# A transformer trunk kernel: narrow and small loads moved to ScalarE's queue, forget logits moved into the gate projection, more warm-up products

## Chip, cores and metric

The kernel runs on one core of a Trainium2 chip. The metric is the device time of one execution in microseconds (us), from its start to its end on that core; the number compared is the median of several runs.

## What is computed

Two layers work on 256 tokens of 2048 channels in float32. The first is attention with a forget gate, the second a causal convolution of 31 taps with layer norm; both have a SiLU gate and a residual. The change touches only the start of the first layer and when the second layer's small parameters are loaded.

```python
proj = h @ w_in                      # h: normed x, w_in: [2048, 4 * 2048 + 16]
q, k, v, gate, f_logit = split(proj) # four blocks of 2048 columns, and 16 forget columns, one a head
log_f = log_sigmoid(f_logit + b_f)
c = cumsum(log_f, axis=1)            # running sum over the tokens
s = q @ k.T * scale + c[:, None] - c[None, :]     # per head, causal
o = softmax(s) @ v
h = h + (o * silu(gate)) @ w_out
```

## The kernel before

Products are made with weights as the stationary operand, 128 x 128, and activations of 256 tokens as the moving one. To keep float32 accuracy each weight tile and each activation tile is split into an upper part (`hi`, ScalarE, L93) and a remainder (`lo`, VectorE or GpSimd, L94), and three products are added: hi*ah, hi*al, lo*ah (L161 with the channels of the result on the partition, L188 to L190 with tokens on it).

Weights come as tiles of 1 MB, 128 partitions x 2048 numbers in runs of 2 KB (`weight_tile`, L105), through SP's queue, into three buffers in turn. A tile's transfer is issued when the `lo` split of the tile that held its buffer is done. Four tiles make a projection of 512 columns, that is four heads. For the first four heads the projections come in the order K, Q, gate, V; below their tiles are called k0 to k3, q0 to q3, g0 to g3 and v0 to v3. A projection has 16 k-tiles, four in a weight tile; a k-tile of K, Q or gate is 12 products.

TensorE runs in the order of the program. Other work is put between the projections' products by an agenda: `at(n, f)` calls `f` n k-tiles later ("step"). In a stretch at the start ScalarE, VectorE and SP are in program order too; outside it these engines are ordered by a planner when the program is built.

At the start `warm_up(n)` puts n float32 products of a matrix of ones on TensorE while x and the first weights are under way. K follows, piece by piece, with the transposes of x between. Then, still in the part that is written out by hand, SP issues q0, the 16 forget columns (`fst`, 2048 rows of 64 bytes), the forget bias (`bf`), four parameter vectors (`prm`), and q1. ScalarE splits q0, sums squares of x, splits q1, and sums squares again; from these come the rows' scales `r0` and, by `row_scales` at step 8 of Q, the tile `rb`.

`load_par` transposes `prm` on TensorE (used by the second layer only). `forget_logits` splits `fst` into `fw`, makes 32 products with it (L396, L397) and scales and biases the result (`zt`). Three steps later `forget_gates` transposes `zt` (`pz`, L409) and computes log-sigmoid on GpSimd in a chain of some 25 small operations, two of them powers (L426, L428), which ends in four copies to `lfn` (L442). `forget_sums` makes the running sums on TensorE (`pc`, L450), split into `chi` and `cc`; GpSimd makes of them `la` and `rbh` (L479 to L482), which the scores of the first head (L485) need right after V.

```python
at(8, load_par)                       # step 8 of Q
at(8, lambda: row_scales(r0, ...))    # step 8 of Q
at(10, forget_logits)                 # step 10 of Q; forget_gates three steps later
...
sil = gate_group(hg)                  # the gate projection
at(4, forget_sums)                    # step 4 of V
```

Of the kernel before, what the change touches and what calls it, by code (L numbers as in the profile page):

```python
# [27 lines left out]
def tile_hybrid_trunk(  # L28
# [28 lines left out]
    # pools that live for a part of the kernel only  # L57
# [21 lines left out]
    # residual stream with the channel on the partition: hT[:, channel tile, token]  # L79
# [16 lines left out]
    def weight_tile(wv, c0, width, g, pieces=1, pool=None):  # L96
        """DMA of kg k-tiles of a column block, [128, kg * width] = 1 MB."""
# [12 lines left out]
    def split_tile(raw, width, lo_engs, hi=None, lo=None):  # L110
        """Exact halves of a weight tile, a piece for each engine in lo_engs."""
# [27 lines left out]
    # work that is interleaved with the projections: (step, function), a step being 12 products of 256 rows  # L139
# [12 lines left out]
    def products_t(ps, kt, hv, lv, ah, al, nts, by_pass=False):  # L152
        """Adds the products of k-tile kt to the given n-tiles of (x @ w)^T."""
# [15 lines left out]
    def proj_t(wv, c0, width, ah, al, lo_engs, pieces=1, banks_apart=False, ahead=False, made=()):  # L169
        """Banks of (x @ w)^T: two n-tiles of [128, 256 tokens] a bank."""  # L170
        ps = banks_t(width)
        tail = []
        for kt, hv, lv in stream(wv, c0, width, lo_engs, pieces, ahead, made):
            if banks_apart and kt >= KT - 2048 // width:
                # the banks end one after the other
                products_t(ps, kt, hv, lv, ah, al, range(2))
                tail.append((kt, hv, lv))
            else:
                products_t(ps, kt, hv, lv, ah, al, range(width // P))
# [4 lines left out]
    def products_n(ps, kt, hv, lv, ah, al, m, first, last):  # L184
        """Adds the products of k-tile kt to the rows of token block m of x @ w."""
# [9 lines left out]
    def rsqrt_mean(ssum, name, eps):  # L195
        """(ssum / D + eps) ** -0.5 for [P, 2]."""
# [9 lines left out]
    # ================= layer 0: forgetting attention =================  # L206
# [14 lines left out]
    def split_act(kt, layer, hi_t, lo_t, src):  # L221
        """Exact halves of channel tile kt times its norm gain."""
# [17 lines left out]
    with tc.manual_schedule(engines={mybir.EngineType.Activation, mybir.EngineType.DVE, mybir.EngineType.SP}):  # L240
# [30 lines left out]
        warm_up(6)  # L271
# [5 lines left out]
        warm_up(2)  # L277
# [30 lines left out]
        # gate weights of the forget logits and their bias  # L308
        fst = ph.tile([P, S], F32, tag="la", name="fst").rearrange("p (k h) -> p k h", h=H)
        nc.sync.dma_start(fst, w_fin[:, :, 4 * D : 4 * D + H])  # L310
        bf = const.tile([P, 1], F32, name="bf")
        nc.gpsimd.memset(bf, 0.0)
        nc.sync.dma_start(bf[0:H], fox_b_f[0].rearrange("(h o) -> h o", o=1))  # L313

        # the rest of the per-channel parameters, channel on the partition
        nc.sync.dma_start(prm[32:80], conv_b_in[0].rearrange("(k p) -> k p", p=P))
        nc.sync.dma_start(prm[80:96], conv_dw_b[0].rearrange("(k p) -> k p", p=P))
        nc.sync.dma_start(prm[96:112], conv_ln_g[0].rearrange("(k p) -> k p", p=P))
        nc.sync.dma_start(prm[112:128], conv_ln_b[0].rearrange("(k p) -> k p", p=P))
# [16 lines left out]
        square_sums(1)  # L336
        ss0 = sm.tile([P, 2], F32, tag="ss", name="ss0")
# [3 lines left out]
    # causal mask for the two diagonal blocks, in the sign of the negated scores  # L341
# [12 lines left out]
    # tri[t, tok block, u] = 1 where token (block * 128 + t) <= u  # L354
# [20 lines left out]
    at(8, load_par)  # L375
# [14 lines left out]
    def forget_logits():  # L390
        fw = hip.tile([P, 2048], F32R, tag="hi", name="fw")[:, 0 : 2 * KT * H].rearrange("p (k c) -> p k c", k=KT)
        split(fw[:, :, 0:H], fw[:, :, H : 2 * H], fst, nc.vector)
        # both halves of the weights in one product: rows h and H + h add up to head h
# [11 lines left out]
    def forget_gates(zt):  # L405
        """log(sigmoid(forget gate)) for [128 tokens, token block, head]."""
# [7 lines left out]
        # log sigmoid(z) = min(z, 0) - log1p(e), e = exp(-|z|), log1p(e) = 2 artanh(e / (2 + e))  # L414
# [23 lines left out]
        # each head in every quarter of the columns  # L438
# [7 lines left out]
    def forget_sums():  # L446
        """Running sums over the tokens, one product with a triangle of ones, split into exact halves."""
# [3 lines left out]
        # the upper half in quarters 0 and 2 of the partitions, the lower one in 1 and 3  # L451
# [7 lines left out]
    # head selectors: sel[p, h] = 1 where p % 32 == h  # L459
# [5 lines left out]
    def attend(hd, qT, kT, vN, sil, t0, t1, t2):  # L465
        """One head: scores and their softmax, its transpose, and the weighted values."""
# [471 lines left out]
```

## Time and profile before

| what | value |
|---|---|
| median of 3 runs | 928.78 us (928.64, 928.78, 932.81) |
| span of the profiled execution | 931.1 us |
| TensorE matmul busy in it | 889.7 us, 96% |
| VectorE busy | 634.3 us, 68% |
| ScalarE busy | 413.5 us, 44% |
| GpSimd busy | 373.9 us, 40% |

The profiled execution has no time of its own beside its span; it lies between the runs' lowest and highest, 2.3 us over their median. Busy shares are means over the whole span, and the change acts in the first 118 us, where transfers, splits and products take turns in setting the pace. Times in the rows are counted from the span's start.

### The profile page before, as it was taken

The numbers are of one execution on the slowest core, as the hardware profiler recorded it, in microseconds if no ns is written. First come the engines' busy times: TensorE is split into PE (matmuls) and PEld (weight loads), VectorE is DVE, ScalarE is ACT, GpSimd is POOL, SyncE is SP. The second block draws the span as 40 slices with busy tenths as digits, with TensorE's granted clock in tenths as the row PEclk, the third lists the DMA queues.
The fourth block names the chain that finished last, engine by engine and source line by source line (L and its number), as shares of the span: only waits on it lengthen the run. The fifth ranks groups of instructions, "written<-read, shape, count | busy, mean of one in ns | idle before, by whom it ended". The sixth has DMA issues, their size and how long they took to land.

```text
span 931.1 us, 15879 instructions
## 1 busy us (share of the span) xinstructions
PE 889.7 (96%) x6642; PEld 856.5 (92%) x6642; DVE 634.3 (68%) x1026; ACT 413.5 (44%) x535; POOL 373.9 (40%) x240
## 2 busy tenths in 40 slices
PE   8899999999999999999999999999889999588996
PEld 8899899989999999989999999999789999477886
DVE  5464564445544554456556889999999999898551
ACT  4453564346434553454445434432434443366531
POOL 3129252103410241022000487888599688622110
PEclk9999999999999999999999999999899999799999
DMA  9999965689798656654456554565355465325532
GB/s 212 169 181 177 244 180 158 182 171 182 145 179 191 177 146 179 186 207 141 150 173 179 190 182 157 164 223 165 107 181 182 136 209 172 119 89 186 178 134 91
DMA packets 101564, 157.71 MB, mean 169 GB/s; under 512 B 4740, under 2 KB 42740, under 8 KB 101364
## 3 DMA queue, kind: packets, MB, share of 16 engines
q1 hardware_dynamic: 101156, 155.63, 62.0%
q8 instruction: 52, 0.85, 0.4%
q10 hardware_dynamic: 336, 1.07, 0.3%
q14 instruction: 20, 0.16, 0.1%
HBM read 154.59 MB, written 2.10 MB: 168 GB/s over the span
## 4 chain that ended last, share of the span: by engine, by line
PE 62%; DVE 29%; issue 2%; DMA 2%; SPq 2%; POOL 1%; ACT 1%; POOLq 0%; DVEq 0%; ACTq 0%
PE pt L161 42%; DVE acc L697 19%; DVE upad L687 4%; PE pv L188 3%; PE pv L190 3%; PE pv L189 3%; PE po L189 2%; PE po L190 2%; PE po L188 2%; DMA raw<-in_fox_w_in_dram 1%; SPq L313 1%; DMA xn<-in_x_dram 1%; PE sc L485 1%; DVE t L780 1%; PE ptr L514 1%
## 5 line engine op out<-in xcount | busy, mean ns | idle before, releaser
L161 PE MATMUL pt<-ah,lo 128*128 128x256 f32 x1472 | 421.2, 286 | 10.4 <-POOL lo L94 9.9
L161 PE MATMUL pt<-ah,hi 128*128 128x256 f32 x1472 | 423.7, 288 | 3.8 <-ACT hi L93 3.8
L161 PE MATMUL pt<-al,hi 128*128 128x256 f32 x1472 | 420.4, 286 | 0.0
L93 ACT ACTIVATE hi<-raw 128x2048 fp32r<-128x2048 f32 (+2 forms) x188 | 271.0, 1464 | 294.2 <-PE pt L161 164.1
L94 DVE TENSOR_TENSOR lo<-raw,hi 128x2048 fp32r<-128x2048 f32 (+1 forms) x136 | 216.3, 1613 | 199.9 <-ACT hi L93 199.9
L161 PEld LDWEIGHTS pt<-ah,lo 128*128 128x128 f32 x1472 | 286.0, 194 | 11.6 <-POOL lo L94 10.7
L161 PEld LDWEIGHTS pt<-ah,hi 128*128 128x128 f32 x1472 | 286.3, 195 | 4.3 <-ACT hi L93 4.2
L161 PEld LDWEIGHTS pt<-al,hi 128*128 128x128 f32 x1472 | 286.4, 195 | 0.0
L94 POOL TENSOR_TENSOR lo<-raw,hi 128x2048 fp32r<-128x2048 f32 (+1 forms) x52 | 223.5, 4318 | 72.8 <-ACT hi L93 72.2
L697 DVE SCALAR_TENSOR_TENSOR acc<-upad,dwT,acc 128x256 f32<-128x256 f32 x480 | 195.7, 477 | 1.4
L161 PE MATMUL pt<-yh,hi 128*128 128x256 f32 x256 | 73.3, 286 | 0.0
L161 PE MATMUL pt<-yl,hi 128*128 128x256 f32 x256 | 72.5, 283 | 0.6 <-POOL yl L94 0.6
L161 PE MATMUL pt<-yh,lo 128*128 128x256 f32 x256 | 72.5, 283 | 0.0
L479 POOL CAST la<-ones 64x256 fp32r<-64x256 f32 x16 | 6.3, 393 | 142.8 <-PE sc L488 138.5
L188 PE MATMUL pv<-hi,ah 128*128 128x512 f32 x128 | 50.1, 391 | 0.0
L161 PEld LDWEIGHTS pt<-yl,hi 128*128 128x128 f32 x256 | 49.1, 192 | 0.8 <-POOL yl L94 0.8
L189 PE MATMUL pv<-hi,al 128*128 128x512 f32 x128 | 49.8, 389 | 0.0
L190 PE MATMUL pv<-lo,ah 128*128 128x512 f32 x128 | 49.8, 389 | 0.0
L161 PEld LDWEIGHTS pt<-yh,hi 128*128 128x128 f32 x256 | 49.1, 192 | 0.0
L161 PEld LDWEIGHTS pt<-yh,lo 128*128 128x128 f32 x256 | 49.1, 192 | 0.0
L687 DVE SCALAR_TENSOR_TENSOR upad<-ea,par,sig 128x256 f32<-128x256 f32 x16 | 39.4, 2497 | 0.4 <-ACT sig L686 0.3
L94 POOL TENSOR_TENSOR yl<-y,yh 128x256 fp32r<-128x256 f32 x15 | 19.8, 1322 | 42.1 <-ACT yh L93 42.1
(240 smaller groups left out, 1030.0 us busy)
## 6 DMA issues: line engine op xcount, KB each, us to landing
raw<-in_fox_w_in_dram SPq DMA_DIRECT2D x60, 1024.0 KB, 6.3
raw<-in_conv_w_in_dram SPq DMA_DIRECT2D x48, 1024.0 KB, 5.2
raw<-in_fox_w_out_dram SPq DMA_DIRECT2D x16, 1024.0 KB, 5.1
raw<-in_conv_w_out_dram SPq DMA_DIRECT2D x16, 1024.0 KB, 5.1
rawk<-in_fox_w_in_dram SPq DMA_DIRECT2D x4, 512.0 KB, 12.2
xn<-in_x_dram SPq DMA_DIRECT2D x3, 512.0 KB, 11.7
rawk<-in_fox_w_in_dram SPq DMA_DIRECT2D x4, 256.0 KB, 7.5
raw<-in_fox_w_in_dram SPq DMA_DIRECT2D x2, 512.0 KB, 15.2
```

Of the source, the lines that this page charges most:

```text
L93: nc.scalar.activation(dst_hi, src, AF.Copy)
L94: lo_eng.tensor_tensor(dst_lo, src, dst_hi.bitcast(F32), op=ALU.subtract)
L161: nc.tensor.matmul(ps[nt // 2][:, (nt % 2) * S : (nt % 2 + 1) * S], w[:, nt * P : (nt + 1) * P], a(kt), start=(kt == 0 and i == 0 and nt % ...
L188: nc.tensor.matmul(ps, ah(kt)[:, ms], hv, start=first, stop=False)
L189: nc.tensor.matmul(ps, al(kt)[:, ms], hv, start=False, stop=False)
L190: nc.tensor.matmul(ps, ah(kt)[:, ms], lv, start=False, stop=last)
L313: nc.sync.dma_start(bf[0:H], fox_b_f[0].rearrange("(h o) -> h o", o=1))
L485: nc.tensor.matmul(sc[:, 0:S], qT[q][:, j, :], kT[k][:, j, :], start=(i == 0), stop=False)
L514: nc.tensor.transpose(out=pt[:, dst * P : (dst + 1) * P], in_=p[:, srcs * P : (srcs + 1) * P], identity=ident)
L687: nc.vector.scalar_tensor_tensor(u[:, TAPS - 1 :], a, bT[:, ct : ct + 1], sig, op0=ALU.add, op1=ALU.mult)
L697: nc.vector.scalar_tensor_tensor(acc, src, w, negs if t == 0 else acc, op0=ALU.mult, op1=ALU.add)
L780: nc.vector.tensor_tensor(t, dall[:, cs, :], rlb.broadcast_to([P, 2, S]), op=ALU.mult)
```

## The change

- `warm_up(6)` becomes `warm_up(8)`, and `warm_up(2)` becomes `warm_up(5)`.
- The loads of `bf`, of the four parts of `prm` and of `fst` leave SP's queue, where they stood between q0 and q1. ScalarE issues them now, after the second pair of its sums of squares, with `fst` last.
- `forget_logits` is moved from step 10 of Q to step 4 of the gate projection; `forget_gates` stays three steps behind it. `load_par` is moved from step 8 of Q to step 14 of the gate projection. `forget_sums` is moved from step 4 of V to step 6.
- Comments are removed; lines that hold only that are left out below.

```diff
-        warm_up(6)
+        warm_up(8)
...
-        warm_up(2)
+        warm_up(5)
...
         q_raw = [weight_tile(w_fin, 0, 512, 0)]
         fst = ph.tile([P, S], F32, tag="la", name="fst").rearrange("p (k h) -> p k h", h=H)
-        nc.sync.dma_start(fst, w_fin[:, :, 4 * D : 4 * D + H])
         bf = const.tile([P, 1], F32, name="bf")
         nc.gpsimd.memset(bf, 0.0)
-        nc.sync.dma_start(bf[0:H], fox_b_f[0].rearrange("(h o) -> h o", o=1))
-        nc.sync.dma_start(prm[32:80], conv_b_in[0].rearrange("(k p) -> k p", p=P))
-        nc.sync.dma_start(prm[80:96], conv_dw_b[0].rearrange("(k p) -> k p", p=P))
-        nc.sync.dma_start(prm[96:112], conv_ln_g[0].rearrange("(k p) -> k p", p=P))
-        nc.sync.dma_start(prm[112:128], conv_ln_b[0].rearrange("(k p) -> k p", p=P))
         q_raw.append(weight_tile(w_fin, 0, 512, 1))
...
         square_sums(1)
+        nc.scalar.dma_start(bf[0:H], fox_b_f[0].rearrange("(h o) -> h o", o=1))
+        nc.scalar.dma_start(prm[32:80], conv_b_in[0].rearrange("(k p) -> k p", p=P))
+        nc.scalar.dma_start(prm[80:96], conv_dw_b[0].rearrange("(k p) -> k p", p=P))
+        nc.scalar.dma_start(prm[96:112], conv_ln_g[0].rearrange("(k p) -> k p", p=P))
+        nc.scalar.dma_start(prm[112:128], conv_ln_b[0].rearrange("(k p) -> k p", p=P))
+        nc.scalar.dma_start(fst, w_fin[:, :, 4 * D : 4 * D + H])
...
-    at(8, load_par)
...
-            at(10, forget_logits)
...
         qk_evict(qT, ps, -float(P) ** -0.5)
+        if hg == 0:
+            at(4, forget_logits)
+            at(14, load_par)
         sil = gate_group(hg)
         if hg == 0:
-            at(4, forget_sums)
+            at(6, forget_sums)
```

## Rows read from the trace of the kernel before

**Rows 1.** The page: each engine's busy time, share of the span and instructions.
```profile
PE 889.7 (96%) x6642; PEld 856.5 (92%) x6642; DVE 634.3 (68%) x1026; ACT 413.5 (44%) x535; POOL 373.9 (40%) x240
```

**Rows 2.** Busy time by stretch: PE, PEld, DVE, ACT, POOL, granted clock, DMA share, GB/s.
```profile
36.00:39.00 3.00, 2.46 (x18) 2.05 (x17) 2.04 (x4) 2.70 (x5) 0.00 (x0) 1.00 0.17 26
...
56.00:94.70 38.70, 38.70 (x325) 38.34 (x324) 18.84 (x23) 14.65 (x16) 27.49 (x39) 1.00 1.02 179
94.70:117.40 22.70, 22.70 (x103) 18.78 (x102) 13.95 (x10) 11.98 (x10) 4.32 (x5) 1.00 0.99 254
117.40:931.00 813.60, 779.45 (x5879) 752.19 (x5877) 572.92 (x938) 358.40 (x456) 328.94 (x170) 0.98 0.58 165
```

**Rows 3.** SP's queue in order of time: start, us, queue, line, operation, tile.
```profile
21.53 1.30 SPq L310 DMA_DIRECT2D fst<-in_fox_w_in_dram  x1
22.88 13.20 SPq L313 DMA_DIRECT2D bf<-in_fox_b_f_dram  x1
...
38.05 1.81 SPq L105 DMA_DIRECT2D raw<-in_fox_w_in_dram  x3
```

**Rows 4.** ScalarE in order of time: splits of q0, q1, g0, g1; one sum of squares.
```profile
36.30 2.19 ACT L93 ACTIVATE hi<-raw 128x512 fp32r<-128x512 f32 x4 [3.32 <-DMA raw<-in_fox_w_in_dram]
...
46.31 2.19 ACT L93 ACTIVATE hi<-raw 128x512 fp32r<-128x512 f32 x4 [5.74 <-DMA raw<-in_fox_w_in_dram]
48.41 1.04 ACT L326 ACTIVATE junk<-xn 128x1024 f32<-128x1024 f32 x1
...
63.70 1.92 ACT L93 ACTIVATE hi<-raw 128x2048 fp32r<-128x2048 f32 x1 [1.29 <-DMA raw<-in_fox_w_in_dram]
69.82 1.91 ACT L93 ACTIVATE hi<-raw 128x2048 fp32r<-128x2048 f32 x1 [4.20 <-DMA raw<-in_fox_w_in_dram]
```

**Rows 5.** TensorE in order of time, between q0's last product and q1's first.
```profile
43.21 0.28 PE L161 MATMUL pt<-ah,lo 128*128 128x256 f32 x1
46.99 0.39 PE L161 MATMUL pt<-ah,hi 128*128 128x256 f32 x1 [3.50 <-ACT hi L93]
```

**Rows 6.** Busy time in a stretch of q1, columns as in rows 2.
```profile
47.70:51.20 3.50, 3.48 (x17) 3.48 (x18) 2.10 (x5) 2.88 (x6) 0.14 (x1) 0.52 1.04 180
```

**Rows 7.** TensorE's groups in 1:8 and in 8.4:13.6: busy us, mean ns, idle before.
```profile
L269 PE MATMUL warm<-ones 128*128 128x128 f32 x16 | 4.0, 431 | 1.1 <-POOL ones L73 1.1
...
L161 PE MATMUL pt<-ah,hik 128*128 128x256 f32 x8 | 2.3, 433 | 0.0
```

**Rows 8.** The chain of work in 40:72: start, us, what.
```profile
55.38 0.21 DVE dg_l L236
...
56.12 2.88 PE pt L161 x24
...
62.63 4.31 PE pt L161 x36
66.95 0.24 PE pz L409 x2
```

**Rows 9.** VectorE in order of time: remainder of g0.
```profile
65.65 2.29 DVE L94 TENSOR_TENSOR lo<-raw,hi 128x2048 fp32r<-128x2048 f32 x1 [0.97 <-ACT hi L93]
```

**Rows 10.** GpSimd in order of time: forget gates, and the first head's operands.
```profile
69.43 5.46 POOL L426 TENSOR_TENSOR fg<-fg 128x32 f32<-128x32 f32 x1
...
89.19 0.66 POOL L442 COPY lfn<-fg 128x32 f32<-128x32 f32 x4
...
113.74 0.41 POOL L482 CAST rbh<-ones 64x256 fp32r<-64x256 f32 x1
```

**Rows 11.** The chain of work in 0:160, V's start to the first scores.
```profile
94.74 0.23 PE pv L188
...
100.21 0.86 PE pc L450 x4
...
117.44 0.35 PE sc L485 x3
```

**Rows 12.** DMA issues in 0:100: times, KB, median us from issue to landing.
```profile
fst<-in_fox_w_in_dram SPq DMA_DIRECT2D x1, 128.0 KB, 15.6
```

## Prediction

> **What bounds the kernel now.** I read the page's busy times first, then busy time by stretch, then SP's, ScalarE's, TensorE's and GpSimd's instructions in order of time, and the chain of work. TensorE is busy for 96% of the span [rows 1]. After the first V projection it is busy for 779 of 814 us [rows 2], and nothing there is changed; all that work hangs on its predecessors and on no fixed time. So the change is worth what it does to the start of the first scores, 117.44 us [rows 11].
>
> Up to there two paces compete. One is TensorE: 24 products take 2.88 us [rows 8], so 0.12 us each, 1.44 us a k-tile, 5.76 us a weight tile. The other is the transfers. The splits of q1 and g1 both start as their data lands, 46.31 and 69.82 [rows 4]: four tiles in 23.5 us, 5.88 us a tile. The DMA engines show a share of 1.02 from 56 to 94.7 us at 179 GB/s [rows 2]. The paces are within 2%, so a lead of TensorE over its data isn't kept for long: what counts is whether the transfers start sooner.
>
> They do stop once. SP issues fst, and its next issue, bf, takes 13.20 us [rows 3]; four small loads follow, and q1 is issued at 38.05, after the split of q0 has begun at 36.30 [rows 4]. In 36 to 39 us the DMA engines' share is 0.17 [rows 2]. TensorE then idles 3.50 us before q1 [rows 5], and in the 3.5 us from 47.70 the granted clock is 0.52, the lower of its two levels, with 17 products where the full clock would make 29 [rows 6].
>
> **The small loads leave SP's queue.** q1 is then issued as soon as its buffer is free, before q0 has landed. q0 itself doesn't land sooner: fst stood behind it in the same queue. So q1's data comes one tile after q0's, 36.30 + 5.88 = 42.2, which is 4.1 earlier. The transfer of fst is still to be made, somewhere behind q1. It landed at 21.53 + 15.6 = 37.1 [rows 3, 12], 0.8 after q0; as some of it lay beside q0, I take 1.0 us of DMA time. Bounds: 0.8, and 3.0, the stretch in which DMA work fades. From q3 on data is then 3.1 us earlier (1.1 to 3.3).
>
> ScalarE now issues six loads. On SP four small ones took 38.05 - 36.08 = 2.0 us and fst 1.30 [rows 3], so about 3.8 us of ScalarE's sequencer. They come behind q1's split and the sums of squares, at 42.2 + 2.19 + 2 x 1.04 [rows 4] = 46.5; q2's data comes at 48.1. They need no data, so I let them run while the sums are executed: 0 us; if each waits for the engine, q2 is split 2.2 us late. ScalarE then has no further load until the output.
>
> The Trainium skill, "DMA: Bandwidth & Descriptors", section "Issuing engines are not separate DMA queues", speaks against the move: queues of different engines end on the same 16 DMA engines, and only issue time is saved. By it the gain would be nothing but the 13.20 us of SP; the sum here has no other gain either.
>
> **More warm-up products.** 16 matmul records of warm-up, two a product, take 4.0 us [rows 7], so 0.5 us each. Five more are 2.5 us, of which some falls into waits for x: K ends up to 2.5 later. On the other side K's first products (8 with the upper parts, and twice as many of the other two kinds) take 433 ns in the mean [rows 7], q0's last one 280 [rows 5]: the lower level. At 3.5 / 17 = 0.206 us [rows 6] instead of 0.12 these 24 lose 2.1 us; at the full clock sooner, K ends up to 2.1 sooner. If sooner, Q still can't start before q0, which lands at 36.30 with ScalarE idle for 3.32 us before it [rows 4]. If later, the wait at `row_scales` (2.2, below) takes it in nearly whole. I take 0, with 0.3 late and 0 early as bounds; with faster transfers that cover goes, and the 2.1 show.
>
> **TensorE's clock through Q and gate, after.** q0's products end at 43.5 as now [rows 5]. q1's data is split from 42.2, so q1 follows at once and at the full clock: 43.5 + 5.8 = 49.3. There `row_scales` waits for VectorE, which now does its second `dg` behind the four remainders of q2 and ends it at 55.6 [rows 8]; q2's data being 4.1 earlier, that becomes 51.5. TensorE, through with q1 at 49.3, waits 2.2 us there (0 if the planner puts `dg` ahead), and goes on at 56.12 - 4.1 = 52.0. Eight k-tiles, with logits and gate transposes gone, bring Q's end to 63.5; now it is 66.95 + 0.24 + 3 x 1.44 = 71.5 [rows 8], of which 59.00 to 62.63 are the logits, 3.63.
>
> g0's data comes at 63.70 - 3.1 = 60.6. A gate tile is split whole: ScalarE 1.92, then VectorE until 65.65 + 2.29 = 67.94 [rows 9], 4.24 after the data. So g0 is ready at 64.8; TensorE, there at 63.5 with two products that need no remainder, waits 1.1. g0 ends at 70.4. Now the logits: their `fw` is split behind g1's remainder, g1's data coming at 66.7, thus 66.7 + 4.24 + 0.4 = 71.3; TensorE waits 0.9. These 3.63 us covered late tiles in Q; here they can't, as they wait themselves. They end at 75.0, three k-tiles bring `pz` to 79.3, nine more and `load_par` (0.1) bring V's start to 92.6. It is 94.74 now [rows 11]: 2.1 gained.
>
> **The forget chain.** From `pz` at 66.95 [rows 8] to the last copy to lfn at 89.85 are 22.9 us, mostly GpSimd, one power alone 5.46 [rows 10]. Now `pc` comes at 100.21 [rows 11], 33.3 us after `pz`, so 10 us are to spare. After the change `pz` is followed by 0.24 + 9 x 1.44 + 0.1 and by six steps of V, which at (100.21 - 94.74) / 4 = 1.37 each are 8.2: 21.5 us. TensorE waits 22.9 - 21.5 = 1.4 us for lfn, with V's remaining products behind it. Bounds: 0 if waits of TensorE in between give the chain time, and 6.0 if VectorE's copy of `pz` stands behind two remainders of 2.29 [rows 9]. Next is `cc`: now the first head's operands are ready at 114.15 [rows 10], 13.1 after `pc` ends; after, V has 117.44 - 101.07 - 2.7 = 13.7 left. That cover is 0.6, so I add nothing, but a late chain reaches the scores.
>
> The sum: V's start 2.1 sooner, 1.4 lost at lfn, so the first scores come 0.7 us sooner. Of the profiled span that is 930.4; of the median, 928.78 - 0.7 = 928.1.
>
> **Rivals.** *The waits don't come.* If data after q1 comes faster than 5.88 us a tile, g0 and the logits don't wait (2.0 back), and with `dg` ahead of the remainders 2.2 more: 0.7 + 4.2 = 4.9 sooner, 923.9. For it: SP's small loads are gone, and 254 GB/s were moved once V ran. Against: 179 GB/s for nearly 40 us before it, at a full share [rows 2]. K's 2.1 could show then too.
>
> *The narrow load comes late.* The forget columns are 2048 runs of 64 bytes, 128 on each of 16 DMA engines; a weight tile has 32 runs on each. Should they take turns run by run with the weights, they need four tiles, 23.5 us from some 46.5: 70.0, just ahead of `fw`'s split. Issued 3.8 later, 3 us of TensorE's time go: 931. That queues of one DMA engine take turns packet by packet is what the Trainium skill says ("DMA: Bandwidth & Descriptors", "Queues, rings and completion order"); no row here has two busy queues.
>
> *ScalarE is held as SP was: slower.* If fst or a load near it holds ScalarE for 13.20 us [rows 3], the split of q2 slips from 48.1 to about 59.7, 11.6 late. The waits at g0 and at the logits (2.0) go under, and the clock falls for one such stretch (1.7 more): 928.1 + 11.6 - 2.0 + 1.7 = 939.4. It decides from a hold of some 7 us on. For it: it happened on SP. Against: fst itself took 1.30; what was held was the load behind it, and here none is behind it.
>
> *The forget chain is the loss:* at its upper bound, 6.0 instead of 1.4, the time is 932.7.
>
> **Chances.** A measurement here tells some 0.5%, 4.6 us, from no change. The forecast, 926 to 930, 0.58; the waits don't come, 0.20, of which 0.16 passes 4.6 us or is helped past it by K; late load or long forget chain, 0.13, nearly all within 0.5%; ScalarE held, 0.09. So faster 0.17, same 0.72, slower 0.11. The range, 923.5 to 932.5, takes in the first rival, the late load and most of the long chain, and leaves out the hold.
>
> **What would show it.** Right: no gap in DMA work at 36 to 39; q1's split near 42 and no idle time of 3.5 us before q1; no stretch at 0.52 near 48; a wait at `bc` of about 2 us, about 1 each at g0 and the logits; `pc` waiting on GpSimd. Wrong: g0's data more than 5 us earlier than 63.7, no wait at `pc`, or ScalarE without a split from 46 to 55.

## The result, and the profile after

The changed kernel takes 936.79 us in the median of six runs (933.62 to 940.54), the kernel before, on the same chip, 928.71 (928.49 to 932.81). The ratio is 1.008, 95% interval 1.0055 to 1.0106: 0.8% slower, and past the upper end of the predicted range. The profiled execution is the one of 937.74 us, with a span of 936.0; the one shown of before took 932.81, its slowest of six. In each the time is the span and some 1.7 us around it. The six runs of before lie low: in five later sets of 23 to 34 runs, on four chips, the same kernel has medians of 931.7 to 932.5 us. Against those 936.79 would be 0.5% slower, and the execution of 932.81 is a usual one.

The page of the changed kernel, busy times, says that the work is the same [rows 1]: 10 more matmul records, and all else within 1.5 us.

```profile
PE 890.3 (95%) x6652; PEld 855.0 (91%) x6652; DVE 634.2 (68%) x1026; ACT 413.0 (44%) x535; POOL 373.4 (40%) x240
```

So something waits. TensorE in order of time, changed kernel: the transpose `pz`, start of V, forget sums, first scores. In brackets is the idle time before an instruction and what ended it.

```profile
82.50 0.30 PE L408 MATMUL pz<-ident,zt 32*128 32x32 f32 x2
...
95.90 0.40 PE L188 MATMUL pv<-hi,ah 128*128 128x512 f32 x1
...
107.29 1.73 PE L449 MATMUL pc<-tri,lfn 128*128 128x256 f32 x4 [3.04 <-POOL lfn L441]
...
123.53 0.52 PE L484 MATMUL sc<-k,q 128*128 128x256 f32 x3
```

In this view the kernel before has its V start at 94.58, `pc` at 100.05 and the first scores at 117.28 (the chain of [rows 11] shows each about 0.16 later). V starts 1.3 us later, then 3.0 us go before `pc`, and the first scores are 6.25 us later. Behind them the two profiled executions are alike: 931.1 - 117.28 = 813.8 us, and 936.0 - 123.53 = 812.5.

Where TensorE waits between 30 and 125 us, changed kernel: what waits, for what, us in total, times, longest.

```profile
PE pt L161 <- ACT hi L93: 3.5, 2, 2.2
PE pc L449 <- POOL lfn L441: 3.0, 1, 3.0
PE pf L395 <- DVE fw L94: 2.4, 1, 2.4
PE pt L161 <- DVE lo L94: 1.1, 3, 0.6
```

That is 10.0 us in sum. Before there were 4.5, of which 3.50 was the wait ahead of q1 [rows 5]. That one is gone, and three others stand in its place: at the logits (`pf`), at the sums (`pc`), and at tiles of Q.

Busy time by stretch, changed kernel, columns as in [rows 2]:

```profile
36.00:39.00 3.00, 1.08 (x6) 0.87 (x7) 1.32 (x3) 1.98 (x4) 0.00 (x0) 1.00 0.98 174
39.41:42.82 3.41, 3.41 (x18) 3.41 (x18) 0.77 (x2) 1.88 (x4) 0.00 (x0) 0.50 1.02 168
47.70:51.20 3.50, 3.50 (x32) 3.50 (x31) 0.93 (x4) 0.23 (x2) 1.07 (x2) 1.00 1.01 187
56.00:94.70 38.70, 35.73 (x297) 34.92 (x295) 19.16 (x24) 14.46 (x15) 17.63 (x14) 1.00 1.03 175
107.67:111.08 3.41, 3.41 (x10) 2.68 (x9) 1.14 (x3) 0.38 (x1) 0.79 (x3) 0.50 0.83 171
```

The change did what it says. From 36 to 39 us the DMA engines' share is 0.98 where it was 0.17, and in the stretch of q1 the granted clock is 1.00 with 32 products, where it was 0.52 with 17 [rows 2, 6]. But the lower of the two levels, 1.2 GHz, now comes twice, for 3.41 us each time: from 39.41, shortly behind a wait of 2.2 us before q0, and from 107.67, at once behind the 3.0 us at `pc`. Half of each, 1.7 us of products, isn't done in it. After the first that costs nothing: TensorE waits for q2's split all the same, 1.23 us at 53.13. After the second nothing waits, and it is lost.

ScalarE in order of time, changed kernel; ACTq is its queue of DMA issues:

```profile
37.02 2.19 ACT L93 ACTIVATE hi<-raw 128x512 fp32r<-128x512 f32 x4 [5.11 <-DMA raw<-in_fox_w_in_dram]
...
43.66 0.63 ACT L93 ACTIVATE hi<-raw 128x512 fp32r<-128x512 f32 x1 [2.37 <-DMA raw<-in_fox_w_in_dram]
...
44.22 1.62 ACTq L332 DMA_DIRECT2D prm<-in_conv_b_in_dram  x1
...
51.05 1.28 ACTq L336 DMA_DIRECT2D fst<-in_fox_w_in_dram  x1
52.45 4.28 ACT L93 ACTIVATE hi<-raw 128x512 fp32r<-128x512 f32 x8 [4.52 <-PE bc_l L237]
61.93 1.91 ACT L93 ACTIVATE hi<-raw 128x2048 fp32r<-128x2048 f32 x1 [5.21 <-DMA raw<-in_fox_w_in_dram]
...
69.71 0.40 ACT L93 ACTIVATE fw<-fst 128x256 fp32r<-128x256 f32 x1
```

q1's data is there at 43.66 instead of 46.31 [rows 4]. The last sum of squares ends at 47.9; the split of q2 starts at 52.45, right behind the last of the six issues. So the issues hold q2's split. They don't set the pace behind it: g0's data is there at 61.93, 1.8 us sooner than before, and in e7 below, where q2 is split 3.4 us sooner than here, at 61.98.

VectorE in order of time, changed kernel:

```profile
69.83 2.29 DVE L94 TENSOR_TENSOR lo<-raw,hi 128x2048 fp32r<-128x2048 f32 x1 [3.66 <-ACT hi L93]
72.04 0.42 DVE L553 SCALAR_TENSOR_TENSOR q<-pt,rb 128x256 f32<-128x256 f32 x1
...
73.37 0.95 DVE L94 TENSOR_TENSOR fw<-fst,fw 128x256 fp32r<-128x256 f32 x1
...
80.53 2.29 DVE L94 TENSOR_TENSOR lo<-raw,hi 128x2048 fp32r<-128x2048 f32 x1 [1.45 <-ACT hi L93]
82.84 0.19 DVE L417 COPY fg<-pz 128x32 f32<-128x32 f32 x1
...
104.87 2.29 DVE L94 TENSOR_TENSOR lo<-raw,hi 128x2048 fp32r<-128x2048 f32 x1 [2.78 <-ACT hi L93]
```

The split of the forget columns stands behind the remainder of g1 and behind four evictions of q, 73.37; TensorE's logits wait for it until 74.38. The copy of `pz` comes right behind another remainder, at 82.84, but that costs nothing, as `pz` itself ends only at 82.80. From there the chain runs on GpSimd, changed kernel, in order of time [rows 10]:

```profile
83.35 0.34 POOL L422 TENSOR_SCALAR fg<-fg 128x32 f32<-128x32 f32 x1 [7.62 <-DVE fg L418]
...
84.42 5.46 POOL L425 TENSOR_TENSOR fg<-fg 128x32 f32<-128x32 f32 x1
...
100.03 2.14 POOL L433 TENSOR_SCALAR fg<-fg 128x32 f32<-128x32 f32 x1
...
104.50 2.73 POOL L441 COPY lfn<-fg 128x32 f32<-128x32 f32 x4
```

It ends at 107.23, where it ended at 89.85 before. `pc` takes it up at once. From `pz` it takes 24.7 us, some 23 before [rows 8, 10]. What is longer is mostly its end: the four copies to `lfn` take 2.73 us beside VectorE's remainder at 104.87, and took 0.66 [rows 10].

### The profile page after: what moved, and what is told of

Read it like the earlier page. It is cut to its first block, busy times and chain, and to the rows that moved or that the text cites. A ratio compares the mean times of both kernels' runs of the same rounds, so it can differ in the third digit from the quotient of the medians.

```text
span 936.0 us, 15896 instructions
## 1 busy us (share of the span) xinstructions
PE 890.3 (95%) x6652; PEld 855.0 (91%) x6652; DVE 634.2 (68%) x1026; ACT 413.0 (44%) x535; POOL 373.4 (40%) x240
## 4 chain that ended last, share of the span: by engine, by line
PE 56%; DVE 29%; DMA 7%; POOL 4%; issue 3%; ACT 1%; SPq 0%; POOLq 0%; DVEq 0%; ACTq 0%
PE pt L161 37%; DVE acc L699 19%; DMA raw<-in_fox_w_in_dram 5%; DVE upad L689 4%; PE pv L189 3%; PE pv L188 3%; PE pv L190 3%; DMA rawk<-in_fox_w_in_dram 2%; PE po L189 2%; PE po L190 2%; PE po L188 2%; ACT hi L93 1%; DVE lo L94 1%; PE sc L484 1%; POOL fg L425 1%
```

## The experiments

One table for all of them, since they answer each other. It has three times of TensorE in the profile (start of V, `pc`, first scores) and the ratio of the times to those of the kernel before on the same chip, as recorded with its interval (it isn't the quotient of the two medians), five rounds each. The row of after is the result above.

| kernel | V | pc | first scores | ratio, 95% interval |
|---|---|---|---|---|
| before | 94.58 | 100.05 | 117.28 | 1 |
| after | 95.90 | 107.29 | 123.53 | 1.008, 1.0055 to 1.0106 |
| e4_forget_only | 99.48 | 109.32 | 123.91 | 1.0062, 1.003 to 1.0095 |
| e5_warm_only | 95.54 | 101.01 | 118.24 | 1.0004, 0.9977 to 1.0031 |
| e2_old_warm | 96.58 | 106.46 | 121.08 | 1.0048, 1.0021 to 1.0076 |
| e9_loads_only | 101.04 | 106.51 | 123.75 | 1.0097, 1.0071 to 1.0123 |
| e1_sums_later | 96.50 | 111.49 | 119.20 | 1.0027, 1.0002 to 1.0051 |
| e8_logits_late | 94.10 | 116.22 | 123.82 | 1.0037, 1.001 to 1.0064 |
| e11_no_wait | 93.51 | 108.50 | 116.21 | 0.9973, 0.9936 to 1.0009 |
| e6_loads_in_k | 94.42 | 99.89 | 117.13 | 1.0022, 1.0001 to 1.0042 |
| e7_small_in_k | 97.92 | 108.92 | 125.13 | 1.0100, 1.0075 to 1.0126 |
| e10_early_in_q | 91.26 | 97.19 | 114.53 | 0.9991, 0.996 to 1.0021 |
| e12_fst_first | 96.97 | 102.44 | 119.67 | 1.0013, 0.9987 to 1.0039 |
| e13_both | 97.14 | 112.13 | 119.84 | 1.0017, 0.9989 to 1.0044 |
| e14_split_q | 92.12 | 99.02 | 116.34 | 0.9982, 0.9956 to 1.0008 |
| e15_split_gate | 96.29 | 111.28 | 118.99 | 1.0005, 0.9981 to 1.0029 |

The last two columns go together: times 930 us, the ratio is within 3.1 us of what the first scores say (e8: 3.4 against 6.5). What follows the first scores differs between profiled executions by some 10 us (808.6 in e5, 818.3 in e1), so of differences below 0.3% the first scores tell more than the ratio. But they are those of one profiled execution each.

**Which part costs.** e4 makes the forget moves alone on the kernel before:

```diff
-    at(8, load_par)
-            at(10, forget_logits)
+            at(4, forget_logits)
+            at(14, load_par)
         sil = gate_group(hg)
-            at(4, forget_sums)
+            at(6, forget_sums)
```

> Kernel before with the moves of logits, parameters' transpose and sums alone; loads and warm-up as before. Theory 1 (the shortened forget chain is the loss): the wait of 2 to 3 us at the sums and the fall of the clock are there too, 4 to 5 us slower than the kernel before, 933. Theory 2 (the loads on ScalarE's queue are the loss): within 1 us of the kernel before.

Measured: 1.0062, and the first scores at 123.91, near the changed kernel's. TensorE's two new waits are there, with all loads still on SP's queue (e4, TensorE in order of time):

```profile
77.95 0.30 PE L395 MATMUL pf<-ah,fw 128*32 128x256 f32 x1 [2.51 <-DVE fw L94]
...
109.32 1.13 PE L449 MATMUL pc<-tri,lfn 128*128 128x256 f32 x4 [1.49 <-POOL lfn L441]
```

The forget moves alone make a loss as large; it needs nothing of the loads. The near equality of the first scores is chance, as the parts differ: V starts 4.9 us later than before (1.3 in the changed kernel), of which 1.9 are there at q1's first product already (48.93 for 46.99), ahead of anything that the edit moves. The wait at `pc` is 1.49, and the fall of the clock that was expected behind it didn't come.

e5 makes the warm-up alone on the kernel before, e2 takes it back from the changed one:

```diff
-        warm_up(6)
+        warm_up(8)
...
-        warm_up(2)
+        warm_up(5)
```

> Kernel before with the new number of warm-up products alone. K ends 1 to 1.5 us sooner. Theory 1: q0's data sets Q's start, so the time stays within 1 us of the kernel before. Rival (K's gain is kept): 1 to 1.5 us faster. Rival (the longer wait before q0 halves the clock): 1.7 us slower.

> Changed kernel with the old number of warm-up products (6 and 2). Theory 1 (K's earlier end only becomes a wait for q0 and a fall of the clock, and both are hidden before q2's split): within 1 us of the changed kernel. Rival (the warm-up products are part of the loss, by the fall of the clock at 39 us): 1.7 us faster than the changed kernel. Rival (they are the one part that helps): 1 to 2 us slower than it.

Measured: 1.0004 and 1.0048. e2's interval overlaps that of the changed kernel, and its first scores are 2.4 us earlier than there, one profile each: in e2's `pc` waits 1.53 us and the clock doesn't fall behind it. So the price at `pc` is some 3 us lower there; whether the edit or the one execution makes that isn't known. No effect of the warm-up can be told from none.

e9 moves the loads alone, to where the change has them, with the logits in Q as before:

```diff
-        nc.sync.dma_start(fst, w_fin[:, :, 4 * D : 4 * D + H])
-        nc.sync.dma_start(bf[0:H], fox_b_f[0].rearrange("(h o) -> h o", o=1))
...
         square_sums(1)
+        nc.scalar.dma_start(bf[0:H], fox_b_f[0].rearrange("(h o) -> h o", o=1))
...
+        nc.scalar.dma_start(fst, w_fin[:, :, 4 * D : 4 * D + H])
```

> Kernel before with the loads moved to ScalarE's queue behind the sums of squares alone; logits at step 10 of Q. Theory 1: fst lands at 62 us or later, step 10 comes at 55: TensorE waits 8 to 12 us at the logits, some of it given back as later tiles are ready by then: 5 to 9 us slower than the kernel before. Rival (the narrow load comes in time, so the move of the logits was not needed): 2 to 4 us faster than the kernel before.

Measured: 1.0097, slower as by the first theory, with a wait of the size that it gave, but not at the logits. `load_par` at step 8 of Q needs `prm`, and stands in TensorE's order ahead of the rest of Q (e9, TensorE in order of time, then busy time by stretch):

```profile
59.46 0.45 PE L371 MATMUL pp<-ident,prm 128*128 128x128 f32 x1 [9.06 <-DMA prm<-in_conv_ln_b_dram]
```

```profile
54.50:64.75 10.25, 5.29 (x25) 5.32 (x26) 2.02 (x6) 1.80 (x4) 0.40 (x1) 0.50 1.07 165
```

The logits would have been next: ScalarE has the forget columns only at 62.9, after 8.7 us without work. So with the loads there, their users can't stay in Q. The two halves of the change hang together: the loads' place needs the forget move, and that move, where it was put, is the loss.

**What in the forget move costs.** Two kernels take the changed one and give the chain more time: e1 has the sums five steps later in V, e8 has the logits four steps later in the gate projection and the sums seven later in V. e11 has the logits two steps later, the gates one step behind them, and the sums five later.

e1, then e8, then e11:

```diff
-            at(6, forget_sums)
+            at(11, forget_sums)
```

```diff
-            at(4, forget_logits)
+            at(8, forget_logits)
...
-            at(6, forget_sums)
+            at(13, forget_sums)
```

```diff
-        at(3, lambda: forget_gates(zt))
+        at(1, lambda: forget_gates(zt))
...
-            at(4, forget_logits)
+            at(6, forget_logits)
...
-            at(6, forget_sums)
+            at(11, forget_sums)
```

> Changed kernel with the running sums at step 11 of V instead of 6. Theory 1 (the forget chain, started in the gate projection, ends 3.0 us after TensorE reaches the sums; the idle time also halves the clock for 3.4 us, 1.7 us of work): both go, about 4.7 us faster than the changed kernel, near 932. Theory 2 (the loss is made before V, by the loads that ScalarE issues and by late data): under 1 us faster, 936 to 937. Theory 3 (the wait moves on to the first scores, since their operands come later): also 936 to 937, with the wait at the scores.

> Changed kernel with the logits at step 8 of the gate projection instead of 4 and the sums at step 13 of V instead of 6. Theory 1 (the logits wait 2.4 us for their weights' split at step 4, and the sums 3.0 us for the chain): both waits go, first scores at 116.5 to 117.5 instead of 123.5, 6 us faster than the changed kernel, about as the kernel before. Rival (a chain that starts later is paid at the first scores, whose operands are late): 0 to 3 us faster than the changed kernel, with a wait at the scores.

> Changed kernel with the logits at step 6 of the gate projection, the gates one step behind them instead of three, and the sums at step 11 of V. Theory 1 (the loss is the wait of 2.4 us at the logits and of 3.0 at the sums with the clock's fall behind it): neither wait is left, V starts near 93.5, first scores near 116, 6 to 7 us faster than the changed kernel and 0 to 1 faster than the kernel before. Rival (the chain's length grows with VectorE's remainders, or a wait moves to the first scores): 3 to 4 us faster than the changed kernel, as with the later sums alone.

Measured, e1, TensorE in order of time:

```profile
111.49 1.02 PE L449 MATMUL pc<-tri,lfn 128*128 128x256 f32 x4
...
119.20 0.52 PE L484 MATMUL sc<-k,q 128*128 128x256 f32 x3
```

e1 has no wait at `pc`, no fall of the clock behind it, and its first scores are 4.3 us earlier than in the changed kernel, though V starts 0.6 later. The wait of 3.04 and the 1.7 of the clock make 4.7 of these 4.9 us, so the two are accounted for. The medians, 934.94 and 936.79, don't show it by themselves. e11 also takes the wait at the logits away and gives the rest back: 116.21, 7.3 earlier than the changed kernel, and the ratio with it (0.9973; the median is 930.52). It changes three steps at once, so the share of each isn't known; what it shows is that no loss is left when neither `fw` nor `lfn` comes last.

e8 missed. Its logits wait 0.22 us and V starts at 94.10, but the chain from `pz` grew to some 30 us (86.46 to 116.18) and `pc` waited 4.26 at 116.22. In the two fences VectorE and then GpSimd in order of time, e8:

```profile
88.18 2.29 DVE L94 TENSOR_TENSOR lo<-raw,hi 128x2048 fp32r<-128x2048 f32 x1 [5.12 <-ACT hi L93]
90.39 0.18 DVE L417 COPY fg<-pz 128x32 f32<-128x32 f32 x1
...
104.34 2.35 DVE L94 TENSOR_TENSOR lo<-raw,hi 128x2048 fp32r<-128x2048 f32 x1 [2.83 <-ACT hi L93]
106.98 2.29 DVE L94 TENSOR_TENSOR lo<-raw,hi 128x2048 fp32r<-128x2048 f32 x1 [0.28 <-ACT hi L93]
```

```profile
104.64 2.13 POOL L433 TENSOR_SCALAR fg<-fg 128x32 f32<-128x32 f32 x1
...
107.20 2.15 POOL L433 TENSOR_SCALAR fg<-fg 128x32 f32<-128x32 f32 x1
```

The copy of `pz` waits 3.6 us in VectorE's order, and each small operation of GpSimd that starts under a remainder ends only with it: 104.64 + 2.13 = 106.77, the remainder 106.69; 107.20 + 2.15 = 109.35, the remainder 109.27. Such an operation takes 0.22 us otherwise. The chain is no fixed 22.9 us, which in the kernel before held one such operation too (2.22 us at 82.40); it takes what VectorE's remainders add to it.

**What the loads' place is worth.** The wait of 3.50 before q1 [rows 5] is gone wherever the loads leave SP's queue. The following kernels look for a place in which they cost nothing. In each, ScalarE issues loads ahead of its work for a k-tile of K, by a table `side` of k-tiles. e6 is the kernel before with the five small loads at k-tiles 1 to 9 and `fst` at 11:

```diff
+        side = {
+            1: (bf[0:H], fox_b_f[0].rearrange("(h o) -> h o", o=1)),
...
+            11: (fst, w_fin[:, :, 4 * D : 4 * D + H]),
+        }
...
         for kt in range(KT):
+            if kt in side:
+                nc.scalar.dma_start(*side[kt])
```

e7 is the changed kernel with the five small loads there and `fst` left behind the sums of squares. e10 is the kernel before with three small loads at k-tile 1, two at 3 and `fst` at 5, and with the steps in Q a little later:

```diff
-    at(8, load_par)
+    at(10, load_par)
...
-            at(8, lambda: row_scales(r0, rb[:, 0, :], "l0"))
-            at(11, lambda: qk_evict(kT, k_banks, 1.0))
-            at(10, forget_logits)
+            at(10, lambda: row_scales(r0, rb[:, 0, :], "l0"))
+            at(12, lambda: qk_evict(kT, k_banks, 1.0))
+            at(11, forget_logits)
```

> Kernel before with the six loads taken off SP and issued one by one by ScalarE between the splits of K (fst last, at k-tile 11); logits, sums and warm-up as before. Theory 1 (taking the narrow load from between q0 and q1 is a gain in itself, and what costs is the place of the logits): q1's data at 42 to 44 us and no 3.5 us wait, logits still covered in Q, first scores near 113, 4 us faster than the kernel before. Theory 2 (data comes at its own pace anyway and the gap on SP's queue costs nothing): within 1 us of the kernel before. Theory 3 (loads on ScalarE's queue hold its splits wherever they stand): K itself slower, 2 to 5 us slower.

> Changed kernel with the bias and the four parameter vectors issued by ScalarE between the splits of K; fst stays behind the sums of squares. Theory 1 (five issues of 1.6 us hold the split of q2 by some 3.4 us): q2 is split at 49 instead of 52.4, the wait of 1.2 us there goes, first scores 1 to 3 us sooner than in the changed kernel. Theory 2 (the forget chain alone sets the first scores): unchanged within 0.5 us, the wait at the sums grows by what was gained.

> Kernel before with the six loads issued by ScalarE early in K (small ones at k-tiles 1 and 3, fst alone at 5), row scales and parameters' transpose at step 10 of Q, K's eviction at 12, logits at 11. Theory 1 (the gain of the loads' move was given back by three waits, for fst, for the rows' scales and by the clock's fall after them): waits of 1.7 and 1.9 us in Q go, V starts near 91 and the first scores come near 113.5, 3 to 4 us faster than the kernel before. Theory 2 (data's own pace sets V's start whatever stands in Q): V's start at 94 as before, within 1 us of the kernel before, with new waits for weight tiles in Q or at g0.

Measured: e6 first (tile `fst`, then TensorE in order of time):

```profile
L304 ACTq DMA_DIRECT2D fst<-in_fox_w_in_dram x1: 403/403/403, 25.5 to 25.5; - x1
...
DMA to landing us min/median/max: 32.1/32.1/32.1
```

```profile
58.62 0.30 PE L397 MATMUL pf<-ah,fw 128*32 128x256 f32 x1 [1.93 <-DVE fw L94]
```

q1 is split from 43.88, 2.4 us sooner than before, but the forget columns take 32.1 us to land beside the weights, the logits wait 1.93, `bc` 1.72, and the first scores are where they were. ScalarE in order of time, e7, the splits of q2, q3 and g0:

```profile
49.00 2.19 ACT L93 ACTIVATE hi<-raw 128x512 fp32r<-128x512 f32 x4 [1.48 <-DMA raw<-in_fox_w_in_dram]
...
54.74 2.20 ACT L93 ACTIVATE hi<-raw 128x512 fp32r<-128x512 f32 x4 [3.54 <-DMA raw<-in_fox_w_in_dram]
...
61.98 1.91 ACT L93 ACTIVATE hi<-raw 128x2048 fp32r<-128x2048 f32 x1 [5.04 <-DMA raw<-in_fox_w_in_dram]
```

q2 is split at 49.00 as e7's first theory said, and TensorE doesn't wait before q2, but g0's data comes no sooner than in the changed kernel. The columns land slowly here too (issued at 43.8, split at 75.5), so the logits start 2.0 us later than there and V with them. Both theories of e7 missed: its first scores are the latest of all, 1.6 us behind the changed kernel's. In e10 the columns land in 17.0 us and TensorE waits nowhere in Q; V starts 3.3 us sooner. But a wait of 3.24 us comes up in K, and the ratio can't be told from 1.

e12 and e13 put the columns fourth from last, with three small loads behind them on ScalarE; e12 has the steps in Q of e10, e13 those of before, and the forget work and `load_par` where e11 has them. The table of both:

```diff
+            1: [(bf[0:H], fox_b_f[0].rearrange("(h o) -> h o", o=1))],
+            3: [(prm[32:80], conv_b_in[0].rearrange("(k p) -> k p", p=P))],
+            5: [(fst, w_fin[:, :, 4 * D : 4 * D + H])],
+            7: [(prm[80:96], conv_dw_b[0].rearrange("(k p) -> k p", p=P))],
+            8: [(prm[96:112], conv_ln_g[0].rearrange("(k p) -> k p", p=P))],
+            9: [(prm[112:128], conv_ln_b[0].rearrange("(k p) -> k p", p=P))],
```

> The kernel before with the six loads issued by ScalarE one by one during K, the forget columns fourth-last (k-tile 5) and three small loads behind them, and with load_par, row_scales, the logits and K's eviction one to three steps later in Q, as in e10. If e10 lost its 3.2 us wait in K, and the half clock behind it, only because five small loads stood ahead of K's tiles, that wait is gone, the forget columns still land before q0 (near 36 us), the first scores come at 112 to 114 us and the median lies 0.3 to 0.5% under that of before (ratio 0.995 to 0.997). If K's tiles themselves set Q's start, the wait moves to Q0 and the first scores stay at 114 to 115 (ratio 0.998 to 1.000).

> The same loads in K as e12, and the forget work placed as in e11: logits at step 6 of the gate projection, gates one step behind, sums at step 11 of V. If the place of the logits is what matters, the logits cover nothing here and a wait in Q (for VectorE's dg) or at g0 comes back: first scores at 114 to 116 us, ratio 0.996 to 1.000, no better than e12. If only the waits matter that e11 removed, it is the best of all: first scores below 113, ratio 0.994 to 0.996.

Measured: both missed, by a wait of 9.1 us in K. ScalarE in order of time, e12, and then TensorE's waits:

```profile
17.34 0.40 ACTq L304 DMA_DIRECT2D fst<-in_fox_w_in_dram  x1
...
18.83 12.01 ACTq L304 DMA_DIRECT2D prm<-in_conv_dw_b_dram  x1
...
30.89 0.47 ACT L224 ACTIVATE ah<-tp,gT 128x256 fp32r<-128x256 f32 x1 [11.07 <-issue]
```

```profile
PE pt L161 <- ACT hik L93: 9.1, 1, 9.1
```

It is what SP did in the kernel before, where the load behind `fst` took 13.20 us to issue [rows 3]; here the queue that is held is ScalarE's, and K's splits with it. That the loss is so small afterwards (1.0013) fits the pace of the transfers: while TensorE stood still, tiles came in, and neither kernel waits again between K and the first scores. That is argued, not shown.

e14 is e12, and e15 is e13, with nothing behind `fst` until q1 is split; in e14 `load_par` goes to step 14 of the gate projection, where e15 has it:

```diff
-            7: [(prm[80:96], conv_dw_b[0].rearrange("(k p) -> k p", p=P))],
-            8: [(prm[96:112], conv_ln_g[0].rearrange("(k p) -> k p", p=P))],
-            9: [(prm[112:128], conv_ln_b[0].rearrange("(k p) -> k p", p=P))],
...
         square_sums(1)
+        nc.scalar.dma_start(prm[80:96], conv_dw_b[0].rearrange("(k p) -> k p", p=P))
+        nc.scalar.dma_start(prm[96:112], conv_ln_g[0].rearrange("(k p) -> k p", p=P))
+        nc.scalar.dma_start(prm[112:128], conv_ln_b[0].rearrange("(k p) -> k p", p=P))
```

> The kernel before with the loads apart: the bias and the first parameter vector issued by ScalarE at k-tiles 1 and 3 of K, the forget columns at k-tile 5 with nothing behind them on ScalarE until q1 is split, and the last three vectors there (load_par moved to the gate projection). Logits stay in Q (step 11, row_scales 10, K's eviction 12). If the 9.1 us wait in K of e12 came from the load behind the forget columns alone, no wait is left in K, they land near 37 us, and the first scores come at 112 to 114 us: ratio 0.993 to 0.997. If the loads' own transfer between K's tiles is the cause, a wait of some us stays in K and the ratio is 0.998 to 1.002.

> The same loads as e14, with the forget work in the gate projection as in e11 (logits at step 6, gates one step behind, sums at step 11 of V). If the place of the logits in itself costs (in Q they fill time in which tiles are late, in the gate projection they come on top), the first scores come 2 to 4 us later than in e14, in which they are in Q. If only the waits counted (for the split of the forget columns and for lfn), which neither has, both give the same first scores within 1 us.

Measured: the wait in K is gone in both, so the load behind the columns was its cause. e14 still missed its 112 to 114: the columns don't land near 37 us (`fst` is issued at 17.15 and 17.34 and lands 32.5 and 31.9 us later, yet in time for both), V starts at 92.12, and `pc` waits 1.26 us. The two differ in the forget work's place and steps, and by two steps of `row_scales` and one of K's eviction, at which neither waits. TensorE in order of time, e14:

```profile
99.02 1.13 PE L450 MATMUL pc<-tri,lfn 128*128 128x256 f32 x4 [1.26 <-POOL lfn L442]
...
116.34 0.52 PE L485 MATMUL sc<-k,q 128*128 128x256 f32 x3
```

and e15:

```profile
65.41 0.39 PE L161 MATMUL pt<-ah,hi 128*128 128x256 f32 x1 [0.96 <-ACT hi L93]
...
67.74 0.39 PE L161 MATMUL pt<-ah,lo 128*128 128x256 f32 x1 [1.82 <-DVE lo L94]
...
118.99 0.52 PE L485 MATMUL sc<-k,q 128*128 128x256 f32 x3
```

g0's data comes at the same time in both, 63.59 and 63.45. With the logits in Q, g0 is there when TensorE wants it; without them it waits 2.78 us at g0, and the granted clock from 69 to 73 us is 0.57. The first scores differ by 2.65 us and the medians by 2.7 (930.35 and 933.07), within the intervals. So in these two profiles the place does cost, as the logits fill time in which a tile is late; the times don't show it. It needn't cost: e11, with its logits in the gate projection and g0's data 1.9 us sooner than in e15, is level with e14 (116.21 and 116.34), with no late logits, no late `lfn` and a granted clock of 1.00 from 57 us to the first scores.

No version is measurably faster than before: e10, e11 and e14 have first scores 2.8, 1.1 and 0.9 us earlier, ratios 0.9991, 0.9973 and 0.9982, and each interval holds 1.

## Why the prediction was wrong

It failed in the forget chain: the step that took 1.4 us at `lfn` and 0.9 at the logits, and added nothing for the clock behind them. Measured were 3.04, 2.37 and 1.7. The waits were the right ones; their sizes, and the price behind one of them, were not. Step by step:

- *SP's small loads, and q1 sooner.* Right in kind. The gap at 36 to 39 us, the 3.50 us before q1 and the low clock in q1 are gone. The size was 1.5 us too good: q1's data was forecast at 42.2 and was there at 43.66, since q0's data came 0.7 later and the tile behind it took 6.6 us instead of 5.88. At g0 and g1 1.8 and 1.9 us of the lead were left, instead of 3.1, within the bounds of 1.1 to 3.3.
- *The narrow load's 1.0 us of DMA time.* Near. Between 58 and 62 us, right ahead of g0's data, 2014 packets passed on ScalarE's queue at a DMA share of 0.35, that is 1.4 us. The second rival's slow landing didn't come; e6 and e7 have it.
- *ScalarE's six issues at 0 us.* Wrong at q2: the four vectors took about 1.6 us each, where SP's had taken 2.0 together [rows 3], and q2's split started at 52.45, some 3.4 us behind its data by e7's 49.00, more than the bound of 2.2. At g0 nothing of it is left, again by e7. It is not the hold of 13.20 us that the third rival feared: nothing stands behind `fst` there. e12 shows that the hold is real on ScalarE as well, and that its condition, as the rival put it, is a load behind.
- *The warm-up at 0 us.* Not contradicted by e5 and e2, and right in its mechanism: K, in the profile shown, was through 1.2 us sooner, TensorE waited 2.2 us before q0, and the clock fell at 39.41. A wait of 1.5 to 2.2 us before q0 is also in e4, e9 and e2, with the old warm-up, so it can't be laid on the new one. The prediction read K's slow first products as the lower level of the clock. They are slow (1.05 us for four, 0.64 in the changed kernel), but the granted clock from 8.4 to 13.6 us reads 1.00 in both kernels, so no row shows that level there.
- *The wait at `bc`, 2.2 us.* It didn't come: VectorE made both `dg` at 49.16, ahead of q2's remainders at 53.11, the other case that the prediction had named.
- *The logits behind g1's remainder, 0.9 us.* Mechanism right, measured 2.37. They started at 74.38 instead of 71.3: g1's data came 1.2 us later than forecast (67.89 for 66.7), the four evictions of q, which the sum left out, stand on VectorE between g1's remainder and `fw`, 1.3 us, and the split itself took 0.95 instead of 0.4. With that, V started 1.3 us later than before, and not 2.1 sooner.
- *`lfn`, 1.4 us.* Mechanism right, measured 3.04, inside its bounds of 0 and 6.0. TensorE's way from `pz` to `pc` was as forecast, 21.75 us for 21.5. The chain took 24.7 us (82.50 to 107.23) instead of 22.9. The reason isn't the one behind the upper bound, a copy of `pz` behind remainders; it is the copies to `lfn` at its end.
- *The clock behind the waits.* Not in the sum. The prediction priced a low clock when it judged the wait before q1, and again in the third rival, but not behind the waits that it forecast itself. At `pc` it costs 1.7 us; e4 and e2, where the wait there is half as long, have none.

The sum: the first scores were forecast 0.7 us sooner and came 6.25 later, 7.0 apart. V's start 3.4, `pc`'s wait 1.6 above its value, the clock 1.7: 6.7 of it. The prediction's fourth rival, the forget chain as the loss, is nearest in its mechanism, with 932.7; it had the place and not the whole price. In number the third, 939.4, is nearer, but its hold didn't happen. e1, e11 and e4 show the place. The medians are 8.1 us apart and the first scores 6.25; as the six runs of before lie 3 to 4 us under its later medians, the first scores are the better measure. What sets the runs of one kernel several us apart stays open. So does the pace of the transfers (some 6 us a tile of 1 MB until V, at a full DMA share), which no kernel here changed.

In e14, with the loads out of SP's way, nothing held and the logits in Q, V starts 2.5 us sooner than before and the first scores 0.9 sooner, near the forecast's 2.1 and 0.7. That is luck and confirms no step: the forecast had the logits in the gate projection and g0's data 3.1 us sooner, and in e14 that data comes at 63.59, for 63.70 before. What e14 shows is what the loads' move can be worth when the logits stay; the changed kernel paid more than that for the logits.

## What to carry to other kernels

Work that TensorE does while a tile is late was free here where it stood; moved to a place where its own operand is late, it costs its wait, and at times the low clock behind the wait: put both into the range, at each wait that you forecast yourself. Where a chain of small operations ends in a wait, count from its start to its user in steps and leave several microseconds, as what other engines put ahead of its links changes from one place to the next. A narrow load held the load issued right behind it for 12 us or more, on either queue, so put it last, or early enough that nothing stands behind it.

## What the hardware showed unasked

- The load right behind 2048 runs of 64 bytes takes 12.0 us to issue on ScalarE's queue (e12, e13) and 13.20 on SP's [rows 3], 14.57 in e4; the narrow load's own issue takes 0.4 to 1.7 us.
- In e14 a small load was issued at 44.72, while `fst` (issued at 17.15, 32.5 us to land) was still under way, and the next only at 49.69, as `fst` landed. The profile shows no cause; it stays open.
- Beside weight tiles on the other queue the narrow load took 31.7 to 32.5 us from issue to landing or split (e6, e7, e14, e15), 17.0 to 19.7 in e10, e12 and e13, and 12.7 in e9. The Trainium skill, "DMA: Bandwidth & Descriptors", "Queues, rings and completion order", says that a DMA engine takes its queues in turn, packet by packet; e14 agrees, with 351 packets on each of the two queues from 30 to 34 us, and so the second rival's mechanism exists. It isn't the whole: in the changed kernel 2014 packets of ScalarE's queue passed between 58 and 62 us beside 276 of SP's. What lets such a burst through stays open.
- A GpSimd operation of 0.22 us that starts under a VectorE remainder ends with the remainder (2.13 to 2.15 us, e8; 2.14 in the changed kernel). The Trainium skill, "Advanced Engine Details and Errata", "GPSIMD Details", says that GpSimd shares a read and a write interface with VectorE and conflicts with its instructions that have two operands in SBUF, as the remainder has; these rows agree.
- The two stretches at 1.2 GHz of the changed kernel (granted clock 0.50) are 3.41 us each, behind waits of 2.2 and 3.0 us; the one of e9 is 10.25 us, 5 us of which are the second half of its wait of 9.06 us. Not each wait is followed by one: in e4, behind those of 2.51 us at the logits and 1.49 at `pc`, the granted clock stays at 1.00 (78 to 82 and 109.3 to 113.5 us). Which waits bring it couldn't be told from these runs.
